# Attention of a hybrid backbone: projections by pairs of heads through DRAM, values two key tiles at a time

## The chip, the cores and the metric

The kernel runs on one core of one Trainium2 chip. The metric is the device time in microseconds (us) of one execution, as the median of several runs. The core has five engines with a queue of instructions each: TensorE (PE, its weight loads PEld), VectorE (DVE), ScalarE (ACT), GpSimd (POOL) and SyncE (SP, which here issues all DMAs). An engine takes its instructions in the order in which the program has them.

## The reference

Two layers run over 1280 tokens (256 of a prompt, 1024 of a sample, which also sees 256 cached keys). Each layer makes one input projection, feeds it to latent attention (8 heads) and to a gated delta rule (GDN, 4 heads, a sequential scan over chunks), gates both, and maps them by one output projection. The change touches the attention:

```
q   = (rmsnorm(q_lat, q_a_norm) @ w_qb).reshape(B, S, H_A, NOPE + ROPE)
q_nope, q_pe = q[..., :NOPE], q[..., NOPE:]            # 64 + 32 per head
ckv = rmsnorm(kv_lat, kv_a_norm)                       # 128 per token, cache appended
kv  = (ckv_all @ w_kvb).reshape(B, -1, H_A, NOPE + V_A)
s = (einsum(q_nope, k_nope) + einsum(q_pe, k_pe)) * scale
o = einsum(softmax(s), v) * silu(g_a)
```

## The kernel before

The program is written as generators ("threads") that record operations. A planner (`Sched`) steps them and decides at build time in which order each engine gets its instructions: it keeps a clock for each engine, takes the thread whose next operation can start first, and breaks ties by the priorities in `PR` (the smaller number goes first). Where the planner's clock has a hole on PE it puts in small filler matmuls (`spare`). The order of the input projection's matrices is the string `ORDER`; of the last `TAIL` matrices token blocks 0 and 1 are done first and block 2 later, so that the buffers of the first blocks come free for the attention.

A layer has three stages. In the first the input projection (`zp`) runs, with the GDN work between. In the second the attention's heads run, with what is left of the GDN scan between. In the third the output projection (`wop`) runs.

For head h, `prep(h)` loads the head's weights (`hw`), multiplies the latent keys and queries (`kp`, `qp`: float32, 64 columns of the array at a time, two blocks side by side), and splits each result into a rounded part hi and a rest lo (ACT and DVE for keys, ACT and POOL for queries). It then finds each query's largest score: 26 matmuls `pm`, each reduced on DVE from PSUM (`at<-pm`), the maxima transposed (`mxt`), scaled on ACT, and sent through DRAM (`mx_d`) into row 96 of the query tile. `main(h)` goes over the key tiles of 128: per tile six `sp` matmuls (hi·hi, hi·lo, lo·hi for two query blocks), an exponential on ACT into `pe`, and, one tile later, the values `po<-pe,vv` (float32, 64 columns, two blocks side by side). POOL and DVE add up the `pe` tiles; at the head's end DVE makes the last addition, and `finish` sums over partitions with two matmuls `pd`, takes the reciprocal, multiplies by the gate on POOL and by `po` on DVE, and writes to DRAM. `prep(h+1)` is paced by flags `m{h}.{tile}` so that its matmuls stand among those of `main(h)`. Key tiles have two slots (`Kt`), and query tiles too (`Q`): head h uses slot h % 2.

Of the kernel before, what the change touches and what calls it, by code (L numbers as in the profile page):

```python
# [16 lines left out]
P = 128  # L17
DM = 1024
# [18 lines left out]
TAIL = 6  # L37
ORDER = 'misc k0 q0 k1 q1 v0 l0 l1 gb0 lk ga0 k2 q2 v1 k3 q3 v2 v3 gb1 gb2 gb3 ga1 ga2 ga3'
PR = dict(ada=2.2, w=2.5, e=2.4, load=2.3, s=1, g=2, p=2.1, kp=2.2, q2=2.2, lat=1, oa=2.45, rope=2.44, prep0=3, prep=3, vv=3, main=4, fin=2, ex=4, red=3, red0=3, prec=5, ldc=4.5, mm=5, fc=1)
VADD = (3, 7, 11)  # L40
# [3 lines left out]
PACE = (0, 0, 0, 1, 2, 3, 4, 4, 5, 6, 7)  # L44
# [12 lines left out]
class Sched:  # L57
# [47 lines left out]
    def run(self):  # L105
        while self.th:
# [115 lines left out]
class Op:  # L222
# [44 lines left out]
    def emit(self):  # L267
        s = self.start()
        if self.eng == "PE":
            n = self.outs[0][0]  # L270
            if (self.half is None) != (Sched.half is None):
                s = max(s, Sched.clk.get("PE", 0.0) + (92 if Sched.half is None else 200))
            if self.half is not None:
                if Sched.half not in (None, (n, self.half)) and Sched.half[0] == n:
                    self.ns = 8
            Sched.half = None if self.half is None else (n, self.half)
# [118 lines left out]
def body(tc, I, O):  # L395
# [74 lines left out]
    qpe_d = dp.tile([2, P, T], F32, name="qpe_d")  # L470
# [88 lines left out]
    def mixer(l, hhl):  # L559
# [315 lines left out]
        def w_thread():  # L875
# [465 lines left out]
        Kt, Q, vvt, at = [], [], {}, {}  # L1341

        def pe_rows(s):
# [3 lines left out]
            ck = bp.tile([P, 2, 32], F32, tag="pe", name="ck", bufs=3) if s else at["ck"]  # L1347
            SY.dma_start(ck, I["cache_kpe"][0, l].rearrange("(c p) f -> p c f", p=P))
# [10 lines left out]
            G.memset(Q[s][1][96:97, :].bitcast(F32), 0.0)  # L1359
            yield 0  # L1360

        def open_attn():
# [5 lines left out]
            o = T + 256  # L1368
            small = t4[:, T:o]
            at.update(ckv=ckv, qn=qn, qr=t4[:, 0:T], hw=[t4[:, o + 192 * i : o + 192 * i + 192].rearrange("p (a b) -> p a b", a=3) for i in range(2)])  # L1370
# [4 lines left out]
            Q.append((t2[:, NK : NK + T], t2[:, NK + T : NK + 2 * T]))  # L1375
            SY.dma_start(ckv[:, 0:T], ckv_d)
            SY.dma_start(qn, qn_d)
            o += 192
            cc = t4[:, o : o + 256].rearrange("p (a b) -> p a b", a=2)
            at["ck"] = t4[:, o + 256 : o + 320].rearrange("p (a b) -> p a b", a=2)  # L1380
            SY.dma_start(cc, I["cache_ckv"][0, l].rearrange("(c p) f -> p c f", p=P))
            sd.add(PR["rope"], rope())
# [6 lines left out]
            yield from pe_rows(0)  # L1389
            sd.add(PR['prep0'], prep(0))  # L1390

        def open_rest():
# [5 lines left out]
            f6 = t6[:, NK:].bitcast(F32)  # L1398
            at["ga"] = [f6[:, 0:640], f6[:, 640:1280]]
            at["ob"] = [bp.tile([P, 512], F32, tag=f"ob{i}", name=f"ob{i}") for i in range(2)]  # L1400
            wv = at["wv"] = bp.tile([P, 512], F32, tag="wv", name="wv")
            SY.dma_start(wv, I["w_v"][l])
            Kt.append((t5[:, 0:NK], t6[:, 0:NK]))
            Q.append((t5[:, NK : NK + T], t5[:, NK + T : NK + 2 * T]))
            for h in range(HA):
                if h:
                    sd.add(PR['prep'], prep(h))
                if h % 2 == 0:
                    sd.add(PR['vv'], vproj(h // 2))
                sd.add(PR['main'], main(h))  # L1410
            sd.add(PR['prec'], pre_c())

        def rope():
# [6 lines left out]
            for g in range(2):  # L1420
# [3 lines left out]
                for b, (c0, n) in enumerate(BLK):  # L1424
# [17 lines left out]
                    SY.dma_start(qpe_d[g, :, c0 : c0 + n], A)  # L1442
# [3 lines left out]
        def vproj(p):  # L1446
            ckv, wv = at["ckv"], at["wv"]
            if p:
                yield f"prep{2*p}"
            vv = vvt[p] = bp.tile([P, NK // P, P], F32, tag="vv", name="vv", bufs=2)  # L1450
            for c0 in (0, 4, 8):
                pt = yield from bank("vp")
                for c in range(4):
                    PE.matmul(pt[:, c * P : (c + 1) * P], ckv[:, (c0 + c) * P : (c0 + c + 1) * P], wv[:, p * P : (p + 1) * P])
# [5 lines left out]

        def prep(h):
            s = h % 2
            ckv, qn = at["ckv"], at["qn"]
            if h:
                yield f"prep{h-1}"
            if h >= 2:
                yield f"main{h-2}"
# [7 lines left out]
            for k0 in (0, 768):
                pt = yield from bank("kp")
                for j in range(2):
                    PE.matmul(pt[64 * j : 64 * j + 64, :384], hw[:, 2, :], ckv[:, k0 + 384 * j : k0 + 384 * j + 384])
                yield 0
                for j in range(2):  # L1480
                    S.copy(kh[0:64, k0 + 384 * j : k0 + 384 * j + 384], pt[64 * j : 64 * j + 64, :384])
                for j in range(2):
                    sl = slice(k0 + 384 * j, k0 + 384 * j + 384)
                    V.tensor_tensor(kl[0:64, sl], pt[64 * j : 64 * j + 64, :384], kh[0:64, sl].bitcast(F32), op=ALU.subtract)
                free(pt)
                yield 0
            hi, lo = Q[s]
            mx, mp = at["mx"][s], at["mp"][s]

            def qproj(bl):  # L1490
                pt = yield from bank("qp")
                for j, b in enumerate(bl):
                    c0, n = BLK[b]
                    for k in range(2):
                        PE.matmul(pt[64 * j : 64 * j + 64, :n], hw[:, k, :], qn[:, k, c0 : c0 + n], start=(k == 0), stop=(k == 1))
                yield 0
                for j, b in enumerate(bl):
                    c0, n = BLK[b]
                    S.copy(at["qr"][0:64, c0 : c0 + n], pt[64 * j : 64 * j + 64, :n])
                free(pt)  # L1500
                for b in bl:
                    c0, n = BLK[b]
                    q = at["qr"][0:96, c0 : c0 + n]
                    S.copy(hi[0:96, c0 : c0 + n], q)
                    G.tensor_tensor(lo[0:96, c0 : c0 + n], q, hi[0:96, c0 : c0 + n].bitcast(F32), op=ALU.subtract)
                yield 0
# [22 lines left out]
            yield from qproj((0,))  # L1529
            yield from mxp(0, 0, 256, mx[:, 0:2], 2)  # L1530
            for b in (1, 2):
                if b == 1:
                    yield from pace(1)
                    yield from qproj((1, 2))
                for t in range(4 * b - 2, 4 * b + 2, 2):
                    for q in (t, t + 1):
                        yield from pace(5 * b - 3 + q - (4 * b - 2))
                        for i, x0 in enumerate((256, 768)):
                            yield from mxp(q, x0, 512, mp[:, q - 2, i : i + 1])
# [370 lines left out]
```

## Time and profile before

| | us |
|---|---|
| median of 3 runs (2219.53 to 2223.38) | 2223.09 |
| profiled execution, its own time | 2217.9 |
| its span, first to last instruction | 2216.1 |
| PE busy | 2097.0 |
| DVE busy | 1442.9 |
| POOL busy | 847.4 |
| ACT busy | 771.0 |

Busy times are unions of instructions of one engine. A matmul's record is longer than the distance to the next matmul, since matmuls are pipelined: what PE needs is read from start to start. A float32 matmul leaves two records. The idle time in brackets stands before an instruction, with the engine or DMA that ended it.

### The profile page before, as it was taken

How to read it: one execution, taken by the hardware profiler on the slowest of the kernel's cores; microseconds unless marked ns; L12 is line 12 of the kernel's file. 1: busy time of each engine (PE TensorE's matmuls, PEld its weight loads, DVE VectorE, ACT ScalarE, POOL GpSimd, SP SyncE). 2: the span in 40 equal slices, each digit the busy share in tenths (PEclk: the TensorE clock that was granted, in tenths of full speed). 3: DMA queues.
4: the chain of work that ended last, by engine and by line, in shares of the span. 5: the costliest groups of instructions: out<-in, count | busy, mean ns of one | idle time of the engine just before them, and what ended most of it. 6: DMA issues, size and time to landing. Idle time of an engine off the chain costs nothing. (4 is left out here: it accounts for less than half of the span.)

```text
span 2216.1 us, 35036 instructions
## 1 busy us (share of the span) xinstructions
PE 2097.0 (95%) x12154; PEld 1519.9 (69%) x12154; DVE 1442.9 (65%) x3085; ACT 771.0 (35%) x2120; POOL 847.4 (38%) x757
## 2 busy tenths in 40 slices
PE   8899999989989998999999999998998999899998
PEld 6676778778666654555777777887876665455576
DVE  4767476686585765564667783887749576665454
ACT  4244224242124344443222441433222434544311
POOL 2343222352415247445331442144341524735521
PEclk9999999989999999999999999999999999999999
DMA  7376776856764322101423654677875441310153
GB/s 276 118 240 196 250 223 194 237 168 209 221 168 150 101 83 71 34 18 50 148 101 95 196 163 151 191 219 216 255 248 158 116 136 53 100 33 19 41 161 110
DMA packets 388481, 327.88 MB, mean 148 GB/s; under 512 B 88736, under 2 KB 326784, under 8 KB 388048
## 3 DMA queue, kind: packets, MB, share of 16 engines
q1 hardware_dynamic: 388304, 325.63, 48.9%
q8 instruction: 97, 1.59, 0.3%
q14 instruction: 80, 0.66, 0.1%
HBM read 220.08 MB, written 105.46 MB: 147 GB/s over the span
## 5 line engine op out<-in xcount | busy, mean ns | idle before, releaser
L312 PE MATMUL zp<-hh,wh 128*128 128x512 f32 (+2 forms) x1128 | 421.5, 374 | 8.4 <-DVE ai L312 6.9
L312 PE MATMUL zp<-hh,wl 128*128 128x512 f32 (+2 forms) x1128 | 421.1, 373 | 4.1 <-POOL wl L312 3.8
L312 PE MATMUL zp<-hl,wh 128*128 128x512 f32 (+2 forms) x1128 | 420.6, 373 | 3.2 <-POOL hl L312 3.1
L312 POOL TENSOR_TENSOR wl<-wr,wh 128x512 fp32r<-128x512 f32 (+1 forms) x114 | 156.2, 1370 | 400.8 <-DVE wh L312 231.5
L312 ACT ACTIVATE pe<-sp 128x512 f32<-128x512 f32 (+1 forms) x352 | 201.6, 578 | 259.0 <-PE sp L312 243.5
L312 DVE TENSOR_REDUCE at<-pm 128x1 f32<-128x512 f32 (+1 forms) x336 | 212.3, 683 | 80.2 <-PE pm L312 79.3
L312 POOL TENSOR_TENSOR pe<-pe,pe 128x1024 f32<-128x1024 f32 x96 | 229.3, 2388 | 80.8 <-DVE pe L312 51.4
L312 PEld LDWEIGHTS zp<-hh,wh 128*128 128x128 f32 (+1 forms) x1128 | 214.1, 190 | 41.9 <-DVE ai L312 7.1
L312 PE MATMUL sp<-at 97*128 97x512 f32 (+1 forms) x704 | 239.9, 408 | 2.6 <-ACT pe L312 1.5
L312 PEld LDWEIGHTS zp<-hh,wl 128*128 128x128 f32 (+1 forms) x1128 | 214.0, 190 | 38.0 <-issue 5.6
L312 PEld LDWEIGHTS zp<-hl,wh 128*128 128x128 f32 (+1 forms) x1128 | 214.2, 190 | 36.3 <-POOL hl L312 4.5
L312 PE MATMUL po<-pe,vv 128*64 128x512 f32 (+1 forms) x768 | 187.1, 563 | 3.4 <-ACT pe L312 2.6
L312 PEld LDWEIGHTS sp<-at 97*128 97x128 f32 x704 | 123.3, 189 | 88.5 <-issue 56.1
L312 POOL TENSOR_SCALAR kpt<-ktok,kdb 128x128 f32<-128x128 f32 x160 | 130.0, 824 | 94.1 <-DMA ai_d<-kpt 84.4
L312 PE MATMUL pm<-at 96*128 96x512 f32 (+1 forms) x416 | 129.2, 385 | 7.9 <-ACT at L312 4.6
L312 PE MATMUL sp<-at,at 97*128 97x512 f32 (+1 forms) x352 | 136.5, 388 | 0.0
L312 DVE TENSOR_TENSOR pe<-pe,pe 128x256 f32<-128x256 f32 (+1 forms) x64 | 79.5, 1244 | 83.9 <-POOL pe L312 43.4
L312 PE MATMUL wop<-woh,ol 128*128 128x512 f32 x288 | 114.4, 397 | 2.2 <-POOL ol L312 2.2
L312 PE MATMUL wop<-woh,oh 128*128 128x512 f32 x288 | 114.5, 398 | 0.0
L312 PE MATMUL wop<-wol,oh 128*128 128x512 f32 x288 | 114.3, 397 | 0.0
L312 PEld LDWEIGHTS pm<-at 96*128 96x128 f32 x416 | 70.9, 191 | 61.5 <-ACT pe L312 21.4
L312 DVE TENSOR_TENSOR wtmp<-blk,W 104x31 f32<-104x31 f32 (+15 forms) x248 | 105.6, 426 | 4.6 <-POOL W L312 0.9
(267 smaller groups left out, 3860.7 us busy)
## 6 DMA issues: line engine op xcount, KB each, us to landing
wr<-in_w_main SPq DMA_DIRECT2D x116, 256.0 KB
ti<-ai_d SPq DMA_DIRECT2D x144, 192.0 KB
ai_d<-ai SPq DMA_DIRECT2D x80, 256.0 KB
kc<-kqv_d SPq DMA_DIRECT2D x160, 128.0 KB
wa<-in_w_ada SPq DMA_DIRECT2D x64, 256.0 KB
kqv_d<-yc SPq DMA_DIRECT2D x48, 256.5 KB
kq<-kqv_d SPq DMA_DIRECT2D x16, 641.0 KB
rb<-grow_d SPq DMA_DIRECT2D x80, 128.0 KB
```

What stands on the lines that cost most here:

```text
L312: op = Op(lambda: f(*a, **k), self.key, self.ns(name, a, k, aps), outs, [x for x in aps if x is not acc])
```

## The change

`proj(p)` now makes keys and queries for a pair of heads at a time, with all 128 columns, splits them in `split` (ACT makes hi; DVE, or POOL where the source isn't PSUM, makes lo) into a staging tile `ev`, and writes both parts to DRAM (`kx_d`, `qx_d`). `loads(h)` reads a head's parts back into its slots. Pair 0 is made with two staging tiles before the heads start, pairs 1 to 3 with one (`at["ev"][:1]`), each from flag `m{2p-2}.5` on. The rotary queries go the same way (`qpe_d` with hi and lo). The hi part of the queries has three slots (`Qh[h % 3]`). `prep(h)` keeps the maxima, now key block by key block. `main` is one thread over all heads; values are multiplied for two key tiles at a time (`PVB`), and a block's `pd` goes with a later group of values than its last one. In `finish` the sums are copied by ACT and the reciprocal is made in pieces of 128. DVE adds one tile (6) and the last of a head, POOL seven. `ORDER` has v0 after lk and ga0 among the tail, and TAIL is 7, so that four more weight tiles are loaded.

```
-TAIL = 6
-ORDER = 'misc k0 q0 k1 q1 v0 l0 l1 gb0 lk ga0 k2 q2 v1 k3 q3 v2 v3 gb1 gb2 gb3 ga1 ga2 ga3'
+TAIL = 7
+ORDER = 'misc k0 q0 k1 q1 l0 l1 gb0 lk v0 k2 q2 v1 k3 q3 v2 v3 gb1 gb2 gb3 ga0 ga1 ga2 ga3'
-VADD = (3, 7, 11)
+VADD = (6,)
+PVB = 2
...
+        def split(x, n):
+            i = at["evn"] = at.get("evn", -1) + 1
+            ev = at["ev"][i % len(at["ev"])]
+            S.copy(ev[:, 0, :n], x)
+            (V if x.space == PSUM else G).tensor_tensor(ev[:, 1, :n], x, ev[:, 0, :n].bitcast(F32), op=ALU.subtract)
+            return ev[:, :, :n].bitcast(F32)
+
+        def proj(p):
+            ckv, qn, hw = at["ckv"], at["qn"], at["hw"]
+            if p:
+                yield "rest"
+                yield f"proj{p-1}"
+                yield f"m{2*p-2}.5"
+            for k0 in range(0, NK, 512):
+                pt = yield from bank("kp")
+                PE.matmul(pt, hw[:, 2, :], ckv[:, k0 : k0 + 512])
+                yield 0
+                SY.dma_start(kx_d[p, :, :, k0 : k0 + 512], split(pt, 512))
+                free(pt)
+            for c0, n in BLK:
...
+                SY.dma_start(qx_d[p, :, :, c0 : c0 + n], split(pt[:, :n], n))
...
+        def loads(h):
+            s, p, g = h % 2, h // 2, h // 4
...
+            if h >= 3:
+                yield f"main{h-3}"
+            yield f"rope{g}"
+            SY.dma_start(qh[64:96].bitcast(F32), qpe_d[g, pe, 0])
+            yield f"proj{p}"
+            SY.dma_start(qh[0:64].bitcast(F32), qx_d[p, rows, 0])
+            for i, (a, b, after) in enumerate(((0, 256, "m{}.0"), (256, 768, "m{}.4"), (768, 1280, "m{}.8"), (1280, NK, "main{}"))):
+                if h >= 2:
+                    yield after.format(h - 2)
+                SY.dma_start(kh[0:64, a:b].bitcast(F32), kx_d[p, rows, 0, a:b])
+                sd.flag(f"kk{h}.{i}")
...
         def prep(h):
-            hw = at["hw"][s]
-            SY.dma_start(hw, I["w_hd"][l, h])
...
             def pace(i):
-                if h:
-                    yield f"m{h-1}.{PACE[i]}"
+                yield f"kk{h}.{i}"
+                if h >= 2:
+                    yield ("m{0}.1", "m{0}.6", "m{1}.0", "m{1}.2")[i].format(h - 2, h - 1)
...
+        def main():
+            todo, done = [], []
+            def pv(n):
+                sums = [b for b in done if b["age"]]
...
+                for x in todo[:n]:
+                    b, kt, m = x["b"], x["kt"], x["b"]["n"]
+                    for y in range(2):
+                        PE.matmul(b["po"][64 * y : 64 * y + 64, :m], vvt[b["h"] // 2][:, kt, b["rows"]], x["pe"][:, y, :m], start=(kt == b["kts"][0]), stop=(kt == b["kts"][-1]))
+                for b in sums:
+                    for y in range(2):
+                        PE.matmul(b["pd"][64 * y : 64 * y + 64, : b["n"]], twos, b["acc"][:, y, :])
...
+                        todo.append(dict(b=blk, kt=kt, pe=pe))
+                        if len(todo) > PVB:
+                            yield from pv(PVB)
```

How PE's order changes is seen first inside a head. Before, in head 5 of the first layer (`at_7079` are its keys and queries, `at_6486` those of head 6, whose maxima `pm` are found meanwhile):

```order
L312 MATMUL sp<-at_7079,at_7080 128x512
L312 MATMUL sp<-at_7079 128x512
L312 MATMUL pm<-at_6486 128x512
L312 MATMUL sp<-at_7079 128x512
L312 MATMUL pm<-at_6486 128x256 x2
L312 MATMUL sp<-at_7079,at_7080 128x512
L312 MATMUL po<-pe,vv 64x512 x2
L312 MATMUL sp<-at_7079 128x512 x2
L312 MATMUL sp<-at_7079,at_7080 128x512
L312 MATMUL sp<-at_7079 128x512 x2
L312 MATMUL sp<-at_7079,at_7080 128x512
L312 MATMUL mxt<-ident,at_6488 10x128
```

A visit to the values (64 columns) came after each key tile, six `sp` apart. Now, in the same head (`at_7352` and `at_7351` are its keys and queries):

```order
L315 MATMUL sp<-at_7351 128x512
L315 MATMUL sp<-at_7352 128x512
L315 MATMUL sp<-at_7352,at_7351 128x512
L315 MATMUL sp<-at_7351 128x512
L315 MATMUL sp<-at_7352 128x512
L315 MATMUL sp<-at_7352,at_7351 128x512
L315 MATMUL sp<-at_7351 128x512
L315 MATMUL sp<-at_7352 128x512
L315 MATMUL sp<-at_7352,at_7351 128x512
L315 MATMUL sp<-at_7351 128x512
L315 MATMUL sp<-at_7352 128x512
L315 MATMUL po<-pe,vv 64x512 x4
```

There are twelve `sp` between visits, each visit has four `po`, and head 6's maxima are no longer among them. In the whole program PE goes into 64-column work and out again 232 times before and 109 times now. The second place is the passage from head 5 to head 6 of the first layer. Before:

```order
L312 MATMUL po<-pe,vv 64x512 x2
L312 MATMUL sp<-at_7079 128x512 x2
L312 MATMUL sp<-at_7079,at_7080 128x512
L312 MATMUL sp<-at_7079 128x512 x2
L312 MATMUL sp<-at_7079,at_7080 128x512
L312 MATMUL po<-pe,vv 64x512 x2
L312 MATMUL vp<-wv,at_6485 128x128 x4
L312 MATMUL po<-pe,vv 64x512 x2
L312 MATMUL pd<-pe_9830,twos 64x512 x2
L312 MATMUL vp<-wv,at_6485 128x128 x8
L312 MATMUL kp<-at_6485,at_6488 64x384 x2
L312 MATMUL sp<-at_6486 128x256 x2
```

Head 6's maxima were complete before head 5's last tile, and its first `sp` follows work that is at hand. Now:

```order
L315 MATMUL sp<-at_7352 128x512
L315 MATMUL po<-pe,vv 64x512 x2
L315 MATMUL pm<-at_6431 128x512 x2
L315 MATMUL po<-pe,vv 64x512 x2
L315 MATMUL pm<-at_6431 128x512 x14
L315 MATMUL pm<-at_6431 128x256 x8
L436 MATMUL spare<-ident 128x128 x30
L315 MATMUL mxt<-ident,at_6433 10x128
L315 MATMUL pm<-at_7351 128x256 x2
L315 MATMUL pm<-at_7351 128x512 x8
L436 MATMUL spare<-ident 128x128 x6
L315 MATMUL sp<-at_6431 128x256 x2
```

All but two of head 6's `pm` now stand behind head 5's last `sp`, then fillers, `mxt`, ten `pm` of head 7, fillers, and head 6's first `sp`. Head 4 has the same form with twelve and six fillers, and the second layer has the same in both places. The third place is SP's queue. Before, at the start of head 5's run:

```order
L312 DMA mx_d0_5_9776<-at4_6488 10x128
L312 DMA at5_7079<-mx_d0_5_9776 1x1280
L312 DMA at4_6488<-in_w_hd 128x192
L312 DMA at4_6488<-qpe_d_101 32x1280
L312 DMA at6_7080<-gates_d_97 64x128
L312 DMA at6_7080<-gates_d_97 64x512
L312 DMA at6_7080<-gates_d_97 64x128
L312 DMA at6_7080<-gates_d_97 64x512
L312 DMA o_d_102<-ob1_7082 64x512 x2
L312 DMA o_d_102<-ob0_7081 64x128 x2
L312 DMA mx_d0_6_10057<-at4_6488 10x128
```

Head 6 needed two loads, weights and rotary queries. Now, in the same stretch (`at2`, `at3` take keys and queries of head 6, `at5`, `at6` of head 7):

```order
L315 DMA at2_6431<-kx_d_102 64x256
L315 DMA at5_7351<-qx_d_103 64x1280
L315 DMA at5_7351<-kx_d_102 64x256
L315 DMA at5_7351<-kx_d_102 64x512 x2
L315 DMA at2_6431<-kx_d_102 64x512 x2
L315 DMA at2_6431<-kx_d_102 64x256
L315 DMA at2_6431<-qpe_d_101 32x1280
L315 DMA at2_6431<-qx_d_103 64x1280
L315 DMA at3_6432<-kx_d_102 64x1536
L315 DMA at5_7351<-kx_d_102 64x256
L315 DMA at5_7351<-qpe_d_101 32x1280
L315 DMA at5_7351<-qx_d_103 64x1280
```

Head 7's keys go into the slot that head 5 is reading, so those loads wait for PE, and the larger part of head 6's keys stands in the queue behind them.

## Rows read from the trace of the kernel before

**Rows 1.** Windows by stage: PE, PEld, DVE, ACT, POOL busy; clock; DMA share.

```profile
624.00:678.00 54.00, 47.16 (x357) 38.33 (x356) 39.02 (x102) 18.13 (x52) 5.30 (x8) 0.97 0.65 177
678.00:1035.00 357.00, 346.22 (x1705) 196.85 (x1703) 213.51 (x341) 164.71 (x350) 185.13 (x110) 0.99 0.24 70
1730.00:2093.00 363.00, 350.10 (x1724) 198.85 (x1724) 215.63 (x342) 165.85 (x356) 185.14 (x112) 0.99 0.25 72
```

**Rows 2.** Timeline of PE in head 5 and 6: start, length, what.

```profile
961.30 1.08 PE L312 MATMUL po<-pe,vv 128*64 128x512 f32 x4
962.30 0.73 PE L312 MATMUL sp<-at 97*128 97x512 f32 x2
962.88 0.40 PE L312 MATMUL sp<-at,at 97*128 97x512 f32 x1
963.11 0.62 PE L312 MATMUL sp<-at 97*128 97x512 f32 x2
963.57 0.40 PE L312 MATMUL sp<-at,at 97*128 97x512 f32 x1
963.89 1.08 PE L312 MATMUL po<-pe,vv 128*64 128x512 f32 x4
964.90 1.16 PE L312 MATMUL vp<-wv,at 128*128 128x128 f32 x8
...
969.84 0.87 PE L312 MATMUL kp<-at,at 128*64 128x384 f32 x4
970.64 0.50 PE L312 MATMUL sp<-at 97*128 97x256 f32 x2
...
974.68 1.03 PE L312 MATMUL qp<-at,at 128*64 128x256 f32 x4
975.63 0.73 PE L312 MATMUL sp<-at 97*128 97x512 f32 x2
...
979.37 1.94 PE L312 MATMUL qp<-at,at 128*64 128x512 f32 x8
981.24 0.72 PE L312 MATMUL sp<-at 97*128 97x512 f32 x2
```

**Rows 3.** Timeline of PE, a float32 product with all 128 columns.

```profile
577.69 1.13 PE L312 MATMUL rp<-at,wpe 128*128 128x256 f32 x4
578.47 0.58 PE L312 MATMUL zp<-hh,wh 128*128 128x512 f32 x1
```

**Rows 4.** Timeline, end of head 2 in the first layer.

```profile
836.90 4.96 POOL L312 TENSOR_TENSOR wol<-wor,woh 128x512 fp32r<-128x512 f32 x4
836.98 7.62 DVE L312 TENSOR_TENSOR pe<-pe,pe 128x1024 f32<-128x1024 f32 x3 [6.92 <-POOL pe L312]
844.32 1.98 PE L312 MATMUL pd<-pe,twos 128*64 128x512 f32 x4 [5.47 <-DVE pe L312]
```

**Rows 5.** Timeline, end of a head in the second layer.

```profile
1897.97 1.97 PE L312 MATMUL pd<-pe,twos 128*64 128x512 f32 x4 [5.26 <-DVE pe L312]
```

**Rows 6.** Instructions by tile: count, duration ns min/median/max, first and last start.

```profile
L312 DVE TENSOR_REDUCE at<-pm x336: 675/681/694, 633.2 to 2056.7; 128x1 f32<-128x512 f32 x128, 128x2 f32<-128x512 f32 x40
L312 DVE TENSOR_TENSOR pe<-pe,pe x64: 361/1224/5956, 685.5 to 2095.9; 128x1024 f32<-128x1024 f32 x48, 128x256 f32<-128x256 f32 x16
L312 POOL TENSOR_TENSOR pe<-pe,pe x96: 2355/2378/2849, 694.9 to 2092.1; 128x1024 f32<-128x1024 f32 x96
L312 ACT COPY vv<-vp x24: 566/585/603, 638.7 to 2025.0; 128x512 f32<-128x512 f32 x24
L312 DVE TENSOR_TENSOR ra<-rp,rt x8: 671/683/693, 582.3 to 1672.3; 128x512 f32<-128x512 f32 x8
```

**Rows 7.** Timeline of the maxima's way into the query tile, head 4, first layer.

```profile
884.05 0.28 PE L312 MATMUL mxt<-ident,at 128*10 128x128 f32 x1
...
884.66 0.30 SPq L312 DMA_DIRECT2D mx_d<-at  x1
...
885.96 0.23 SPq L312 DMA_DIRECT2D at<-mx_d  x1
...
888.33 0.48 PE L312 MATMUL sp<-at 97*128 97x256 f32 x2
```

**Rows 8.** Waits of SP's queue for landings: us in total, times, longest.

```profile
SPq L312 <- DMA mx_d<-at: 16.8, 15, 2.9
SPq L312 <- DMA ai_d<-ai: 8.4, 8, 3.1
SPq L312 <- DMA xs<-x: 6.0, 1, 6.0
```

More of the change, by code (lines that the diff above doesn't have):

```diff
@@ L272, in emit @@
                 s = max(s, Sched.clk.get("PE", 0.0) + (92 if Sched.half is None else 200))
[L273 to L276, printed above, removed]
+            if self.half is None:
+                Sched.half = None
+            elif Sched.half and Sched.half[0] == n and self.half not in Sched.half[1]:
+                self.ns = 8
+                Sched.half[1].add(self.half)
+            else:
+                Sched.half = (n, {self.half})
         e = s + self.ns
@@ L1358, in pe_rows @@
             G.memset(lo[96:97, :].bitcast(F32), 0.0)
-            G.memset(Q[s][1][96:97, :].bitcast(F32), 0.0)
+            G.memset(Ql[s][96:97, :].bitcast(F32), 0.0)
             yield 0
+        def split(x, n):
[17 more added lines that the diff above has]
+            for c0, n in BLK:
+                pt = yield from bank("qp")
+                for k in range(2):
+                    PE.matmul(pt[:, :n], hw[:, k, :], qn[:, k, c0 : c0 + n], start=(k == 0), stop=(k == 1))
+                yield 0
+                SY.dma_start(qx_d[p, :, :, c0 : c0 + n], split(pt[:, :n], n))
+                free(pt)
+            if p + 1 < HA // 2:
+                SY.dma_start(hw, I["w_hd"][l, p + 1])
+            yield 0
+            sd.flag(f"proj{p}")
         def open_attn():
@@ L1389, in open_attn @@
             yield from pe_rows(0)
+            sd.add(PR["rope"], rope())
+            for p in range(HA // 2):
+                sd.add(PR['projs' if p else 'proj'], proj(p))
+            sd.add(PR['prep0'], loads(0))
             sd.add(PR['prep0'], prep(0))
@@ L1475, in prep @@
[L1475 to L1486, printed above, removed]
@@ L1487, in prep @@
-            hi, lo = Q[s]
-            mx, mp = at["mx"][s], at["mp"][s]
[L1490 to L1506, printed above, removed]
+            kh, hi = Kt[s][0], Qh[h % 3]
@@ L1612, in main, with finish @@
                 yield 0
-            sd.flag(f"main{h}")
-        def finish(h, po, acc, m, c0, n, ga):
+        def finish(b):
+            h, c0, n, ga, po, pd = (b[q] for q in ("h", "c0", "n", "ga", "po", "pd"))
             p, e = h // 2, h % 2
             i = at["n"] = at.get("n", -1) + 1
-            if i >= 2:
-                yield f"ob{i-2}"
-            pd = yield from bank("pd")
-            for x in range(2):
-                PE.matmul(pd[64 * x : 64 * x + 64, :n], twos, acc[:, x, :n])
-            yield 0
-            ob = at["ob"][i % 2]
-            V.reciprocal(ob[:, :n], pd[:, :n])
+            j = i % len(at["ob"])
+            ob, rc, user = at["ob"][j], at["rc"][j], at.get(("user", j))
+            at["user", j] = f"ob{i}"
+            if user:
+                yield user
+            V.tensor_tensor(ob[:, :n], po[:, :n], ga, op=ALU.mult)
+            free(po)
+            S.copy(rc[:, :n], pd[:, :n])
@@ L1626, in finish @@
             free(pd)
             yield 0
-            G.tensor_tensor(ob[:, :n], ga, ob[:, :n], op=ALU.mult)
+            for x in range(0, n, P):
+                V.reciprocal(rc[:, x : x + P], rc[:, x : x + P])
+                yield 0
+            G.tensor_tensor(ob[:, :n], ob[:, :n], rc[:, :n], op=ALU.mult)
             yield 0
-            V.tensor_tensor(ob[:, :n], po[:, :n], ob[:, :n], op=ALU.mult)
-            free(po)
             for x in range(2):
@@ L1641, in pre_c @@
             yield f"done{HB-1}"
+            yield "rest"
             gs.close()
+            b2 = open_pool(bs, f"b2{l}", bufs=1, side="right")
+            for t in ("ob", "rc"):
+                at[t].append(b2.tile([P, 512], F32, tag=t, name=t))
             cw = open_pool(cs, f"cw{l}", bufs=1)
```

228 lines of the change are left out of this document (122 added, 106 removed).

## The prediction

> **What bounds the kernel now.** I read the windows by stage first. In both attention stages PE is busy in 97% and 96% of the stretch (346.22 of 357.00, 350.10 of 363.00), and DVE, POOL and ACT in 46% to 60% [rows 1]. So the attention is bound by PE, and the change is worth what it takes off PE's path, less the waits that it puts there. The 54 us in front of the first attention stage have 7 us without PE [rows 1].
>
> Then I read PE's own order from start to start. Two `sp` stand 0.46 us apart from the next two (963.11 to 963.57), 0.23 each. From one visit to the values to the next, with six `sp` between, it is 2.59 us (961.30 to 963.89) [rows 2]. Six times 0.23 is 1.38, so the visit costs 1.21. Its arithmetic is 0.86: eight `qp` records take 1.87 (979.37 to 981.24), four `po` records 1.01 (963.89 to 964.90), and the second four add the difference [rows 2]. Hence 0.35 us of each visit is passage: 0.09 on the way in (0.32 from the last `sp` to `po` instead of 0.23), 0.15 on the way out (1.01 instead of 0.86), and 0.12 at the first two `sp` (0.58 instead of 0.46) [rows 2].
>
> Last I looked for PE's long holes in the attention. The two longest are `pd` waiting for DVE's last addition of a head, 5.47 and 5.26 us [rows 4, 5].
>
> **The change part by part.** The sum is made against the profiled execution, 2217.9 us (span 2216.1).
>
> Visits. PE goes into 64-column work 232 times before and 109 times now, 123 fewer. At 0.34 (0.35 is from 512-column visits, some are shorter) that is 41.8 us less, nearly all in the two stages where PE is the bound. Bounds: only the way out, 0.15, saves 18; all of 0.36 (0.09 + 0.15 + 0.12) saves 44.
>
> Projections. Keys cost the same: before, two visits a head of 0.80 less the way out, 0.65 each, so 1.30 [rows 2]; now three products of 512 with all columns, 0.86 each, serve two heads, 1.29 a head. Queries cost 0.95 - 0.15 = 0.80 plus 1.87 - 0.15 = 1.72, together 2.52 a head [rows 2]; now one product of 256 (two halves, 0.78 [rows 3]) and four of 512 at 0.86, 4.22 a pair, 2.11 a head. Sixteen heads save 6.6 us. The way into and out of full-width float32 seems free: 0.78 holds both [rows 3]. Bounds 0 and 6.6.
>
> The sums `pd`. They now go with a later group of values, some ten `sp` on, about 2.3 us at the least and in most heads longer, and behind them stands work of the next head. The holes of 5.47 and 5.26 go, 10.7 us; what is late next is `finish`, which has a whole head for it. In rows: DVE's addition starts at 836.98 beside four POOL instructions from 836.90 on [rows 4] and takes up to 5956 ns instead of 1224 [rows 6]. The Trainium skill, "SBUF — State Buffer", section "SBUF: two separate sides", calls the port pair of VectorE and GpSimd an exclusive lock: who starts first holds it for the instruction and the other blocks. The rows agree: DVE finished only behind POOL's run. By that rule DVE's delay stays, since `wol` and seven additions a head are POOL's, and if the maxima's reduces behind it held PE as long, this term would be 0; by the rows PE waited for `pd` alone, so I keep 10.7 and 0 as the other bound.
>
> Loads and staging. This is what is added. From the middle of head 2p-2, six blocks go through one staging tile: ACT 0.59, DVE 0.68 [rows 6], a write to DRAM, and only then the next block's ACT copy. No row has a write of 512 KB with its landing alone. The nearest waits are 2.9 us at the longest for a small write, 3.1 for one of 256 KB and 6.0 for one of 512 KB [rows 8]; I take 3.1, and with 0.5 for the passes between engines a block takes 4.9 us and a pair 29. From head 4's first `sp` to head 6's it is 82.3 us (888.33 to 970.64 [rows 2, 7]), 41 a head, now some 38; so with 19 us of head 2p-2 left, pair p is ready about 10 us into head 2p-1.
>
> Idle at head 6. In SP's queue the larger part of head 6's keys stands behind loads into head 5's slot, which wait until PE has read head 5's tile 9. From there: SP issues and a landing, 3.4 us (2.4 is the longest that a small read can have taken, 885.96 to 888.33 [rows 7], and 1.0 for issues); twenty reduces of 0.68, 13.6 [rows 6], with 3 us of DVE's other work between; `mxt` to the first `sp`, 4.3 (884.05 to 888.33 [rows 7]). That is 24.3 us. PE has in it two key tiles (12 `sp`, 2.8), two visits with four `po` (4.1), 26 `pm` (16 at 0.23 and ten half as long, 4.9) and ten `pm` of head 7 (2.1): 13.9. So about 10 us are idle. Before, all of this lay beside head 5's matmuls.
>
> Idle at head 4. Its key loads come a step earlier, so only four reduces and the way of the maxima stand open: 2.7 + 0.2 + 4.3, less 3.1 of `pm`, is 4.1; ahead of it two more sets of fillers among head 4's first `pm` mark a hole behind the projection, for which I take another 4. Head 2 has GDN work to fill. So 18 us a layer, 36 in all. Bounds: 9 (in both places only the way of the maxima, 4.3 less 2.1 of `pm`) and 60 (10 at each of heads 2, 4 and 6).
>
> Costs at nothing. DVE makes one pe addition of 1.22 fewer a head, the reciprocals and splits come to about the same; POOL's one more of 2.38 [rows 6] takes the place of the three query splits that it loses; ACT does less: all stay near 60% of a shorter stage. SP gets 178 more DMAs in the whole run, at some 0.3 us of issue (0.30, 0.23 [rows 7]), nearly all in stages whose DMA engines are 24% busy [rows 1]; what that costs is the order, counted above. Four more weight tiles and v0 four matrices later lie beside `zp`, which fills PE. Pair 0's products replace head 0's; I take 0 for the passage, with 7 either way, the idle time there.
>
> Sum: 2217.9 - 41.8 - 6.6 - 10.7 + 36 = 2194.8. The median of the runs shown, 2223.09, is 5.2 above the profiled execution; on that footing the forecast is 2200.
>
> **The rivals.**
> First, the new idle time is small: DVE and SP run ahead of the planner's clock, and only 9 us stay. 2200 - 27 = 2173. For it: DVE has 40% free. Against: the queue's order is fixed, and the reduces' 13.6 us cannot start sooner.
>
> Second, the passage is cheaper and DVE stays locked: visits save 25 (0.20 each, between 0.15 and 0.34), `pd` nothing. 2223.1 - 25 - 6.6 + 36 = 2227, about no change. For it: the period also holds reduces' and exponentials' waits. Against: the same 0.32 and 1.01 stand at both visits shown [rows 2].
>
> Third, slower: the staging tile. If a write takes the 6.0 us of [rows 8], a block takes 7.8 and a pair 47, 18 us later. Each of the two exposed heads a layer starts that much later, four times 18 = 72: 2272. It decides from 23 / 4, some 6 us a pair or 1 us a block, on. For it: ACT and DVE take the block's copies in order among exponentials and reduces, and I gave that 0.5. Against: the 6.0 is a single wait [rows 8]; here the DMA engines are at 24% [rows 1].
>
> That the visits don't become fewer is no rival: PE's order shows it.
>
> **How the numbers follow.** The forecast, 2200 (2183 to 2216), gets 0.48; the first rival, below 2183, 0.19; the second, 2216 to 2234, 0.16; the third, above, 0.17. This measurement tells 0.2% from no change, 4.4 us. Faster than 2218.6: 0.48 + 0.19 + 0.05 of the second = 0.72. Within: 0.09. Slower than 2227.5: 0.19. The range for 8 in 10 goes from 2168, a little under the first rival, to 2242, part of the third's way.
>
> **What would show it.** Right: some 345 us instead of 357 from the first `sp` to the first `wop` of a layer, and 350 instead of 363 in the second; visits of eight `po` records in about 2.1 us; no `pd` with more than 1 us idle before it; idle of 4 and 10 us before `mxt` and the first `sp` of heads 4 and 6, with DVE in reduces without a break, and SP waiting for PE. Wrong: `po` visits of over 2.4 us; ACT held at the staging tile for more than 5 us a block; idle time also at heads 2, 3, 5 or 7; or a first attention stage that starts much later than at 678.

## The result, and the profile after

The changed kernel takes 2248.6 us (median of 4 runs, 2245.3 to 2254.1), before 2222.5 in the same series: ratio 1.0127, 95% interval 1.0103 to 1.0151. It is slower by some 26 us; 2200 (2168 to 2242) was forecast. The profiled execution spans 2244.3 us, 28.2 more than before.

I cut both spans at the start of the last `zp`, the first `sp` and the first `wop` of the first layer, and at the start of the first and last `zp`, the first `sp` and the first `wop` of the second; the pieces of a row add up to the span. What stands ahead of the first `zp` counts to the first stage.

| kernel | first `zp` stage | passages, last `zp` to first `sp` | `zp`, second layer | attention, both | output, both | span |
|---|---|---|---|---|---|---|
| before | 623.7 | 54.4 + 54.1 | 511.0 | 720.0 | 252.8 | 2216.1 |
| after | 616.1 | 74.4 + 61.8 | 523.2 | 708.8 | 260.0 | 2244.3 |

The attention stages got 11 us shorter, and 39 are lost outside them: 28 in the passages, 12 in the second `zp`, 7 in the output projections, less 8 in the first `zp`. Some 10 of the 28 are waiting: in the passages PE idles 16.8 us instead of 12.5 and runs fillers for 11.3 instead of 5.8. The rest is work that moved. All rotary products `rp` stood beside `zp` before; now half of them, 19 us of PE, stand behind the last `zp`. The 12.4 us of keys and queries that stood there before went ahead of it, and some GDN products came over from the attention. The line of `rp` in before, then its windows in the two passages of after:

```profile
L312 PE MATMUL rp<-at,wpe x80: 377/592/697, 577.7 to 1671.3; 128*128 128x512 f32 x64, 128*128 128x256 f32 x16
```
```profile
616.00:690.50 74.50, 10.65 (x20) 4.52 (x20) 2.75 (x4) 0.37 (x1) 0.93 0.87 243
1702.00:1763.80 61.80, 8.33 (x20) 3.56 (x20) 2.76 (x4) 0.37 (x1) 0.96 0.90 241
```

The windows of the two attention stages, to be laid beside [rows 1], and behind them the fillers alone (the line of `spare`: length, PE and PEld busy, clock, DMA share, GB/s):

```profile
690.00:1045.00 355.00, 339.31 (x1670) 216.16 (x1671) 196.96 (x332) 145.45 (x311) 178.53 (x93) 0.98 0.41 118
1763.00:2117.00 354.00, 339.14 (x1713) 216.26 (x1713) 197.98 (x340) 144.55 (x307) 179.01 (x96) 0.98 0.43 121
```
```profile
690.00:1045.00 355.00, 23.20 (x160) 22.78 (x160) 0.98 0.41 118
1763.00:2117.00 354.00, 17.14 (x122) 16.92 (x122) 0.98 0.43 121
```

PE's busy share hides the loss, since fillers count as busy and a low clock makes work look longer. So I split a stage into idle time (length less busy), fillers, time lost to the clock ((1 - granted clock) times length), and the rest, PE's own work. The clock column has two digits, so each clock term is good to about 2 us. Of before, the fillers of the two stages are 6.75 and 4.66.

| attention, both layers | length | idle | fillers | clock | lost in all | PE's own work |
|---|---|---|---|---|---|---|
| before | 720.0 | 23.7 | 11.4 | 7.2 | 42.3 | 677.7 |
| after | 709.0 | 30.6 | 40.3 | 14.2 | 85.1 | 623.9 |

The work fell by 54, and 43 came back as lost time. The visits look as forecast: PE's timeline in head 5 (as [rows 2]) has eight `po` records in 1.87 us, 0.32 from the last `sp` to `po`, and 0.34 from the first `sp` behind them to the next:

```profile
957.33 0.61 PE L315 MATMUL sp<-at 97*128 97x512 f32 x2
957.88 1.94 PE L315 MATMUL po<-pe,vv 128*64 128x512 f32 x8
959.75 0.50 PE L315 MATMUL sp<-at,at 97*128 97x512 f32 x1
960.09 0.64 PE L315 MATMUL sp<-at 97*128 97x512 f32 x2
```

The lost time stands where the next pair begins. PE's timeline from the end of head 5 to head 6's first `sp`, with DVE's maxima beside it:

```profile
969.09 8.77 PE L315 MATMUL pm<-at 96*128 96x512 f32 x22
977.66 7.82 PE L436 MATMUL spare<-ident 128*128 128x128 f32 x60
985.32 0.27 PE L315 MATMUL mxt<-ident,at 128*10 128x128 f32 x1
985.34 2.95 PE L315 MATMUL pm<-at 96*128 96x256 f32 x10
988.13 1.50 PE L436 MATMUL spare<-ident 128*128 128x128 f32 x12
989.39 0.49 PE L315 MATMUL sp<-at 97*128 97x256 f32 x2
```
```profile
968.56 12.04 DVE L315 TENSOR_REDUCE at<-pm 128x1 f32<-128x512 f32 x20
980.64 0.18 DVE L315 TENSOR_REDUCE at<-at 128x8 f32<-128x24 f32 x1
```

A line of a timeline can merge two sizes: the 22 `pm` are 14 of 512 columns and eight of 256, the next ten are two of 256 and eight of 512. The 22 take 8.6 us at DVE's pace (12.04 / 20 = 0.60 us a reduce) instead of 4.2 at 0.23 and half of it, the fillers 7.7 and 1.3, the ten 2.8 instead of 2.1: some 14 us without use. For 4.5 of them the fillers hold PE beyond their cause: the maxima were done at 980.82, and `mxt` stands behind the fillers until 985.32.

Why so late? PE's first `sp` of head 4 and first product of pair 3, ACT's first pass of each block of the pair through the one staging tile, and SP's loads behind the last block:

```profile
902.28 0.35 PE L315 MATMUL sp<-at,at 97*128 97x256 f32 x1 [0.25 <-DVE at L315]
...
918.68 1.12 PE L315 MATMUL kp<-at,at 128*128 128x512 f32 x2
```
```profile
919.85 0.59 ACT L315 CAST at<-kp 128x512 fp32r<-128x512 f32 x1 [0.78 <-PE kp L315]
926.75 0.58 ACT L315 CAST at<-kp 128x512 fp32r<-128x512 f32 x1
932.43 0.58 ACT L315 CAST at<-kp 128x512 fp32r<-128x512 f32 x1
938.08 0.37 ACT L315 CAST at<-qp 128x256 fp32r<-128x256 f32 x1
943.72 0.59 ACT L315 CAST at<-qp 128x512 fp32r<-128x512 f32 x1 [0.28 <-PE qp L315]
950.20 0.59 ACT L315 CAST at<-qp 128x512 fp32r<-128x512 f32 x1 [1.32 <-PE qp L315]
```
```profile
955.91 0.49 SPq L315 DMA_DIRECT2D at<-qx_d  x1
956.50 2.47 SPq L315 DMA_DIRECT2D o_d<-ob  x4
959.01 0.60 SPq L315 DMA_DIRECT2D at<-kx_d  x1
959.65 0.60 SPq L315 DMA_DIRECT2D at<-qx_d  x1
960.60 3.65 SPq L315 DMA_DIRECT2D at<-kx_d  x6
```

A block takes 6.1 us ((950.20 - 919.85) / 5). The pair starts 16 us into head 4, which now lasts only 30 us, and its last block has landed when SP reads it back at 955.91, some 23 us into head 5 (first `sp` at 932.35). From there SP issues the loads of heads 6 and 7 one behind the other, with no pause of more than 0.4 us: none of them waits for PE.

Head 4 is no better. There the first hole is a wait for the keys' landing, with a low clock behind it (0.62 granted from 870 to 875); 24 and 12 more filler records follow:

```profile
867.24 0.77 PE L315 MATMUL pm<-at,at 96*128 96x256 f32 x2 [3.33 <-DMA at<-kx_d]
...
870.01 4.22 PE L436 MATMUL spare<-ident 128*128 128x128 f32 x20
...
896.75 0.28 PE L315 MATMUL mxt<-ident,at 128*10 128x128 f32 x1 [2.73 <-DVE at L315]
```

The `pd` holes of [rows 4, 5] are gone from the heads. One of more than 1 us is left, where a head's last sum stands among the output projection of the second layer:

```profile
2125.10 1.08 PE L315 MATMUL pd<-pe,twos 128*64 128x512 f32 x4 [2.91 <-DVE pe L315]
```

### The profile page after: what moved, and what is told of

Same layout as the page of the kernel before. It is cut to its first block, busy times and chain, and to the rows that moved or that the text cites. A ratio compares the mean times of both kernels' runs of the same rounds, so it can differ in the third digit from the quotient of the medians.

```text
span 2244.3 us, 35296 instructions
## 1 busy us (share of the span) xinstructions
PE 2101.7 (94%) x12158; PEld 1570.2 (70%) x12158; DVE 1438.6 (64%) x3105; ACT 739.7 (33%) x2052; POOL 858.1 (38%) x741
## 4 chain that ended last, share of the span: by engine, by line
PE 41%; DVE 15%; DMA 12%; issue 3%; POOL 3%; SPq 3%; ACT 2%; DVEq 0%; POOLq 0%; ACTq 0%
PE wop L315 9%; PE sp L315 7%; PE po L315 6%; PE zp L315 6%; DVE at L315 3%; SPq L315 3%; PE pm L315 2%; DVE wtmp L315 2%; DVE W L315 2%; POOL pe L315 2%; DVE yc L315 2%; DMA at<-kx_d 1%; PE px L315 1%; DMA wr<-in_w_main 1%; DMA qx_d<-at 1%
## 5 line engine op out<-in xcount | busy, mean ns | idle before, releaser
L315 POOL TENSOR_TENSOR pe<-pe,pe 128x1024 f32<-128x1024 f32 x112 | 267.5, 2388 | 283.3 <-PE po L315 213.4
L315 PE MATMUL sp<-at 97*128 97x512 f32 (+1 forms) x572 | 196.3, 400 | 1.2 <-DVE ob L315 0.9
L315 PE MATMUL sp<-at,at 97*128 97x512 f32 (+1 forms) x484 | 186.9, 410 | 1.3 <-ACT vv L315 0.9
L315 PE MATMUL po<-pe,vv 128*64 128x512 f32 (+1 forms) x704 | 163.0, 578 | 0.3 <-ACT pe L315 0.2
L315 PEld LDWEIGHTS sp<-at 97*128 97x128 f32 x572 | 103.8, 190 | 35.6 <-issue 16.6
L315 PEld LDWEIGHTS sp<-at,at 97*128 97x128 f32 x484 | 91.5, 190 | 34.7 <-issue 11.3
L315 DVE SCALAR_TENSOR_TENSOR yc<-zp_sb,cwh,yc 128x256 f32<-128x256 f32 (+1 forms) x144 | 103.6, 719 | 4.1
L315 PE MATMUL wop<-woh,ol 128*128 128x512 f32 x256 | 101.9, 398 | 1.6 <-POOL ol L315 1.6
L315 PE MATMUL wop<-woh,oh 128*128 128x512 f32 x256 | 102.0, 398 | 0.0
L315 DVE RECIPROCAL rc<-rc 128x128 f32<-128x128 f32 x80 | 70.0, 920 | 47.7 <-ACT rc L315 47.6
```

Of the source, the lines that this page charges most:

```text
L315: op = Op(lambda: f(*a, **k), self.key, self.ns(name, a, k, aps), outs, [x for x in aps if x is not acc])
```

## The experiments

In the names, `a_` is the kernel after with one edit or several, `b_` the kernel before with one; `a_pE` has the projections earlier. The medians are of 4 to 10 runs, and the ratio is to before in the same series.

| kernel | median us | ratio to before, 95% interval | passages | `zp`, layer 2 | attention |
|---|---|---|---|---|---|
| a_oldorder | 2262.8 | 1.0195 (1.0155 to 1.0234) | 81.2 + 77.4 | 516.6 | 709.7 |
| b_neworder | 2256.0 | 1.0147 (1.0118 to 1.0176) | 43.1 + 52.4 | 524.1 | 763.0 |
| a_rope | 2255.0 | 1.0143 (1.0112 to 1.0173) | 68.5 + 58.2 | 535.7 | 697.7 |
| a_pvb1 | 2247.6 | 1.0112 (1.0074 to 1.0149) | 73.9 + 60.2 | 527.8 | 710.8 |
| a_pE | 2217.6 | 0.9975 (0.9958 to 0.9991) | 74.3 + 62.5 | 523.7 | 671.5 |
| a_pE_pvb1 | 2236.1 | 1.0060 (1.0038 to 1.0081) | 74.8 + 59.9 | 524.0 | 697.0 |
| a_pE_tail6 | 2197.3 | 0.9884 (0.9861 to 0.9907) | 62.8 + 61.0 | 526.2 | 658.0 |
| a_ev2x | 2240.6 | 1.0078 (1.0051 to 1.0104) | 74.4 + 62.5 | 534.7 | 704.1 |
| a_tail6 | 2252.8 | 1.0145 (1.0110 to 1.0180) | 64.2 + 58.9 | 525.8 | 710.6 |
| a_mxq | 2255.2 | 1.0156 (1.0124 to 1.0187) | 73.9 + 65.3 | 520.5 | 715.5 |
| a_pE_t6_ld1 | 2203.4 | 0.9920 (0.9892 to 0.9948) | 58.9 + 55.4 | 525.2 | 670.4 |
| a_nofill | 2254.3 | 1.0154 (1.0125 to 1.0184) | 73.0 + 62.6 | 530.2 | 705.4 |
| a_ev1 | 2295.1 | 1.0321 (1.0279 to 1.0362) | 94.8 + 104.9 | 516.9 | 709.0 |
| a_pE_t6_proj | 2186.5 | 0.9823 (0.9791 to 0.9856) | 59.5 + 67.1 | 525.2 | 643.2 |

**The order, in both kernels.** `ORDER` and `TAIL` exchanged between the two kernels.

> The kernel after with ORDER and TAIL of the kernel before (v0 and ga0 early, tail of 6), all else as changed. Theory A (the order is what the start of the attention lost): the first sp comes back from 690.5 and 1763.8 us to about 680 and 1732, and the time falls from 2248.6 to some 2220 to 2225. Theory B (the way of pair 0 and of the rotary queries through DRAM is what it lost): the order is worth nothing, the first sp stays within 5 us of 690 and 1764, and the time stays at 2243 to 2254. Theory C (the heads themselves lost it): as B, no change ahead of the first sp.

> The kernel before with ORDER and TAIL of the kernel after, nothing else. Theory A: the time rises from 2222.5 to some 2240 to 2250, with the first sp 12 us later in layer 0 and 30 us later in layer 1, and the stages between the first sp and the first wop unchanged. Theory B and C: 2218 to 2228.

No theory came out. The kernel before gets some 32 us slower with the new order, more than theory A's price and not in its way: the first `sp` of layer 0 comes 19 us earlier, not later, the passages get 13 shorter, and the attention, which was to stay, 43 longer. The kernel after gets 14 slower with the old order, where theory A had it faster and the others the same. The two don't add: the order is worth a loss of some 32 in one program and a gain of 14 in the other. The second `zp` goes the same way both times: 511.0 becomes 524.1, and 523.2 becomes 516.6. So much of its 12 us goes with the order; but with one and the same order the other edits put it anywhere from 516.9 to 535.7, so the order isn't all of it. The passages follow the rest of the change: 108.5 and 95.5 with the old way of pair 0, 158.6 and 136.2 with the new.

**The rotary queries first.** `sd.add(PR["rope"], rope())` moved back to where the kernel before has it.

> The kernel after with the thread of the rotary queries added where the kernel before adds it (ahead of the key rows and of pair 0's projections). Theory B: the 52 fillers and the 3.3 us wait for wpe at 616 to 626 us go, as does part of the same wait in layer 1, and the time falls by 9 to 20 us, to 2229 to 2240. Theory A: the rotary products only change places with other work, 2243 to 2254. Theory C: as A.

Theory B's price is refuted. What it names is real, as PE's timeline of after shows behind the last `zp`:

```profile
616.32 5.97 PE L436 MATMUL spare<-ident 128*128 128x128 f32 x52
625.60 2.05 PE L315 MATMUL rp<-at,wpe 128*128 128x256 f32 x4 [3.32 <-DMA wpe<-in_w_qpe]
```

The passages get 9.5 shorter, but the first `zp` ends 10 later and the second takes 12 more: of the 40 rotary records in the passages 8 are left, and the work stands beside `zp` again. With them gone the passages are still 18 us longer than before the change.

**The price of a visit.**

```
-PVB = 2
+PVB = 1
```

> The kernel after with PVB = 1: values for one key tile at a time again, some 230 visits to 64-column work instead of 109, and fewer fillers at heads 4 and 6 (216 in all instead of 271). With 0.34 us a visit, as the prediction had it, the attention stages get some 42 us longer, less some 16 us of idle time that goes at heads 4 and 6: 2274. With 0.20 us a visit (what the stage of after suggests: 24 us fewer in po for 120 visits fewer): 25 less 16, 2257. If the idle time at heads 4 and 6 is what eats the gain altogether, 2248 or below.

The third case: 92 visits more (201 instead of 109) cost nothing. Its windows of the attention, and the fillers:

```profile
688.00:1038.00 350.00, 339.52 (x1612) 199.56 (x1611) 191.07 (x333) 146.21 (x311) 178.16 (x93) 0.99 0.42 119
1758.00:2119.00 361.00, 346.28 (x1658) 202.02 (x1656) 192.80 (x341) 144.57 (x303) 175.85 (x96) 0.98 0.42 119
```
```profile
688.00:1038.00 350.00, 12.56 (x100) 12.04 (x100) 0.99 0.42 119
1758.00:2119.00 361.00, 9.48 (x72) 8.82 (x72) 0.98 0.42 119
```

Idle 25.2, fillers 22.0, clock 10.7: 57.9 lost instead of 85.1, and 653.1 of work instead of 623.9. So a visit costs 29.2 / 92 = 0.32 us of PE's work, and the holes had hidden all of it.

**The projections earlier.**

```
-                yield f"m{2*p-2}.5"
+                yield f"m{max(2*p-3,0)}.{0 if p==1 else 4}"
```

> The kernel after with the projections of pairs 1 to 3 set free earlier: flag m0.0 for pair 1 and m{2p-3}.4 (the head before, tile 6) for pairs 2 and 3, instead of m{2p-2}.5. Theory D (the holes ahead of heads 4 and 6 are the end of the pair's chain projection, DRAM, maxima, which starts too late): idle time, fillers and low clock of the two attention stages fall from 85 us to some 45, heads 3 and 5 take about 48 and 43 us instead of 63 and 57, and the time falls by 35 to 50 us, to 2200 to 2213. Theory E (the holes come from head 6's key loads behind head 7's in SP's queue, and from the reduces on DVE, whenever the pair is ready): at most 10 us, 2238 to 2250.

Theory D, with 31 us in place of 35 to 50. The windows and fillers:

```profile
693.00:1021.00 328.00, 315.67 (x1523) 194.43 (x1519) 200.35 (x331) 143.96 (x311) 176.67 (x93) 0.99 0.46 127
1741.00:2084.00 343.00, 323.91 (x1590) 198.82 (x1589) 202.53 (x341) 145.69 (x312) 177.57 (x97) 0.98 0.44 125
```
```profile
693.00:1021.00 328.00, 2.21 (x16) 2.01 (x16) 0.99 0.46 127
1741.00:2084.00 343.00, 0.39 (x2) 0.30 (x2) 0.98 0.44 125
```

Idle 31.4, fillers 2.6, clock 10.1: 44.1 lost instead of 85.1, nearly as little as before the change, with the same work (626.9). Heads 3 and 5 of layer 0 take 44.6 and 33.5 us instead of 63.0 and 57.0. Theory E's price is refuted. The planner makes the order of every queue anew, SP's too, so this run alone doesn't part the earlier start from the new order; that no load of SP waits for PE in the lines of after above speaks against SP's queue as well.

> The kernel a_pE with PVB = 1, values for one key tile at a time. If the visits cost what PE's own times say once no hole hides them (some 29 us of work between the two kernels with and without, 0.24 us a visit), it is 25 to 33 us above a_pE. By the prediction's 0.34 it would be 42 above. If another chain than PE's bounds the heads (as with the late projections, where PVB = 1 cost nothing), it is within 8 us of a_pE.

18.5 above a_pE: less than either price, but far from free. With 97 more visits (207 instead of 110) the attention is 25.5 longer, 0.26 us a visit; the other stages give some of it back. Once the chain is early, PE bounds the heads again and the visits pay.

**The staging tile.** Pairs 2 and 3 get a second tile in the place of the second `ob` and `rc`:

```
-            for t in ("ob", "rc"):
-                at[t].append(b2.tile([P, 512], F32, tag=t, name=t))
+            at["ev"].append(b2.tile([P, 2, 512], F32R, tag="ev2", name="ev2"))
```

> The kernel after with a second staging tile for pairs 2 and 3 from the end of the GDN work on, in the place of the second pair of tiles ob and rc. Theory D': it is the one staging tile that makes the chain late (a block every 6 us): pair 3 takes some 18 us instead of 34, the hole ahead of head 6 goes, that ahead of head 4 stays, and the time falls by 10 to 20 us, to 2228 to 2238. Theory E: within 5 us of after.

Head 5 falls from 57.0 and 57.4 to 45.8 in both layers, as theory D' says, and head 3 stays at 63.5 and 59.8. Of these 23 us 8 are left, under the 10 to 20 expected: the last heads, which lost a tile, take 31.9 instead of 27.9, the second `zp` is 11 longer, the output projections, without the last head's `po` and `pd`, 11 shorter.

**The tail.** `TAIL = 6`, first with the early projections (a_pE_tail6), then alone (a_tail6):

> The kernel a_pE with TAIL = 6 (four weight tiles fewer are loaded and split, block 2 of ga0's neighbour done early), order of matrices as changed. If the longer tail is what made the input projection of the second layer 12 us longer, 8 to 15 us below a_pE, with zp of layer 1 at some 512 us; if it is not, within 5 us of a_pE.

> The kernel after with TAIL = 6 alone. Theory F (the tail of 7 is a loss by itself, whatever the heads do, as a_pE_tail6 against a_pE suggests with its 20 us): 15 to 25 us below after, 2224 to 2234, with the first sp of layer 0 near 684. Theory G (the 20 us came from how the shorter tail meets the early projections): within 8 us of after, 2240 to 2257.

With them it gives 20 us, and not in the second `zp` (526.2), so that reason is refuted; alone it gives nothing (theory G). The gain over a_pE is in the first passage (11.5) and in the attention (13.5).

**SP's queue.** In after, head 0's maxima are scaled at 673.3 and their write is issued at 681.5, behind 11 other DMAs. In a_mxq ACT issues it:

```
+            Q = AD if h < 2 else SY
+            Q.dma_start(md.rearrange("o (t f) -> (o t) f", f=P), mt)
+            Q.dma_start(hi[96:97, :].bitcast(F32), md)
```

> The kernel after with the way of the maxima through DRAM (mx_d, its write and its read) issued by ACT instead of SP for heads 0 and 1; the order of every other instruction stays. Theory H (the start of the attention is late because head 0's maxima stand behind 11 other DMAs in SP's queue, 8.2 us in layer 0 and 3.1 us in layer 1): the first sp comes some 8 us and 3 us earlier and the time falls by 8 to 14 us. Theory I (PE reaches the first sp only after the GDN products that stand ahead of it, and these wait for their own loads): first sp within 3 us of 690 and 1764, the time within 5 us of after.

The timeline of a_mxq:

```profile
671.68 0.56 ACTq L315 DMA_DIRECT2D mx_d<-at  x1
673.01 0.23 ACTq L315 DMA_DIRECT2D at<-mx_d  x1
...
687.53 0.50 PE L315 MATMUL sp<-at 97*128 97x256 f32 x2
```

The maxima's read is issued 11 us earlier than in after (684.23), and the first `sp` comes 3.0 and 1.5 earlier, since GDN products stand ahead of it on PE until 687.5: theory I for the first `sp`. So in after head 0's maxima hold up the first `sp` by 3 us at most. The time is 6.6 up, outside its 5; the second attention stage got 9 longer, and I can't say why.

On a_pE_tail6, head 1's loads were then held back (`yield "m0.0"` in `loads(1)`; a_pE_t6_ld1):

> The kernel a_pE_tail6 with head 1's loads held back to head 0's first tile (flag m0.0), so that SP issues some nine DMAs fewer ahead of the first sp, where it issues 67 to 72 per cent of the time in after. If SP's queue is what holds up the GDN loads there (theory J): the first sp 3 to 6 us earlier in each layer, and the time 4 to 12 us below a_pE_tail6. Otherwise within 5 us of it.

The passages are 9.5 shorter, the attention is 12 longer, the whole 6 slower. Theory J is refuted in its total.

**The fillers.** Left out between the start and the end of the heads (`Sched.spin` does nothing there):

> The kernel after without the filler matmuls from the start of the heads to their end (120 instead of 271 in all; every other instruction keeps its order). Theory K (at head 6 the 30 fillers hold PE 4.5 us beyond the last maximum in each layer, and 6 more stand ahead of its first sp): 9 to 13 us below after, 2235 to 2240. Theory L (without them the granted clock falls in the holes, and what follows runs at the low level): the holes get shorter by as much, but the clock's loss in the attention stages rises from 16 us to 25 or more, and the time stays at 2244 to 2258.

Theory L, by its time and by the clock: without fillers the clock falls. The same ten microseconds at head 6, first of after, then of this kernel:

```profile
980.00:990.00 10.00, 9.90 (x78) 8.92 (x77) 4.92 (x10) 0.27 (x1) 0.00 (x0) 1.00 0.06 18
```
```profile
980.00:990.00 10.00, 6.95 (x24) 5.34 (x22) 9.00 (x16) 1.04 (x3) 0.00 (x0) 0.56 0.12 34
```

Head 5 gets 4.4 and 4.9 shorter, while the stages' clock is 0.94 and 0.96 (35 us lost, 21 more than in after). So the fillers held PE, and leaving them out gained nothing.

**The start of the attention.** One staging tile from the start on (`at["ev"]` without its second tile), and the order of its two users turned round (`proj=2.0` instead of 2.445, on a_pE_tail6; a_pE_t6_proj):

> The kernel after with one staging tile instead of two ahead of the heads too (rotary queries and pair 0 share it); what follows has one tile already. Theory M (the way of pair 0 and of the rotary queries through the staging tiles sets the passage from the input projection into the heads): some 18 blocks wait for one tile, 2 to 3 us more each: both passages get 15 to 40 us longer (from 74 and 62 us), and the time rises by 30 to 70 us, to 2280 to 2320. Theory I (GDN products and their loads set the passage): within 10 us of after.

> The kernel a_pE_tail6 with pair 0's projection ahead of the rotary queries in the planner's priorities (2.0 instead of 2.445). If pair 0's blocks waiting behind the rotary ones for the two staging tiles are what makes the passages long (theory M): 5 to 15 us below a_pE_tail6, both passages shorter by 3 to 8 us. If all blocks of both are needed in any order: within 6 us of a_pE_tail6.

One tile makes the passages 20 and 43 us longer, the first `zp` 12 and the second 6 shorter, and the time 46 longer: theory M's price, the 43 a little above it. With one tile the staging carries the passage; that it does with two isn't shown by this. The second is the fastest of all, 10.8 under a_pE_tail6, but not for theory M's reason: the passages are 3 longer, and the attention is 15 shorter.

```profile
688.00:1010.00 322.00, 312.63 (x1503) 194.42 (x1501) 191.30 (x325) 141.73 (x295) 173.94 (x92) 0.98 0.47 130
1735.00:2057.00 322.00, 315.44 (x1564) 193.93 (x1561) 197.69 (x336) 142.50 (x296) 175.13 (x94) 0.99 0.48 133
```

Idle 15.9, clock 9.7, almost no fillers: 26 lost. PE's own work, 618, is nearly that of after; what went is the lost time. The attention is 77 us shorter than in before, and the kernel is faster than both: 2186.5, with before at 2223.0 in the same series.

## Why the prediction was wrong

**Visits and projections: right.** 41.8 and 6.6, 48.4 together, were forecast; the attention's own work fell by 53.8 (head 1's products, now made with pair 0 ahead of the heads, and some GDN products, now in the passages, are a part). a_pvb1 gives 0.32 us of PE's work a visit where the rows gave 0.34. Once PE bounds the heads, a_pE_pvb1 against a_pE gives 0.26 in the attention and some 0.2 in the whole time. So the price of PE's work was right; the second rival's 0.20 is too low for it, but near what the whole time paid.

**The sums `pd`: nearly right.** 10.7 forecast; the holes are gone from the heads, 2.9 and 0.7 came back at the output projections. The case by the Trainium skill's rule of the lock ("SBUF — State Buffer", section "SBUF: two separate sides"), 0, didn't come. The trace agrees with the rule itself: DVE's additions, which answer to the second line of [rows 6], still stretch beside POOL's work, up to 3357 ns instead of 5956, but no sum in the heads waits for one; the longest is the one behind the 2.9 us:

```profile
L315 DVE TENSOR_TENSOR pe<-pe,pe x32: 1161/1224/3357, 716.0 to 2121.7; 128x1024 f32<-128x1024 f32 x32
```

**Idle time at heads 4 and 6: mis-sized, the first step that failed.** Forecast were 36 more, or 25 with the `pd` holes that go; measured are 43 more lost. The failing step is "pair p is ready about 10 us into head 2p-1": it is 23. A block takes 6.1 us, not 4.9, which is 8 us a pair, and head 2p-2 lasts 30 us, not 38, which leaves 14 us of it instead of 19, since the maxima that had stood in it now stand behind head 2p-1. Around the holes themselves stand two costs that had no term, fillers that hold PE beyond the last maximum (4.5 us at head 6, though a_nofill, without them, was no faster) and the lower clock (7 us more). a_pE shows the cause: only the flag that starts the pairs is moved, and 41 of the 43 are gone; a_ev2x, where a second tile has pair 3's last block read back at 944.45, 9 us into head 5, takes 11 us off head 5 in both layers. Not SP's queue behind head 5's slot, as I had put it, but the pair's late end decided: no load of heads 6 and 7 waited for PE there. That the planner's new order around the earlier flag has no part in the 41 isn't shown.

**The third rival** named this chain. By its own arithmetic 1.2 us a block is 7 a pair and 28 in four places, 2228; the staging was given too little weight, though not as the whole of the loss.

**"Costs at nothing": the second step that failed, and the larger one.** The passage stood at 0, 7 either way, and four weight tiles and v0 at 0. Measured are 39 us outside the attention: 28 in the passages, 12 in the second `zp`, 7 at the output, 8 gained in the first `zp`. The prediction's own sign of error, a first stage much later than at 678, came: 690.5. The step took pair 0's products to replace head 0's in the passage. They don't: they went ahead of the last `zp`, and in their place came half of the rotary products, which the sum nowhere had; a_rope shows the exchange from the other side. Why so many rotary products come behind the last `zp` is shown in part: with one staging tile instead of two, which they share with pair 0, it is 28 records a passage instead of 20, and the passages are 20 and 43 longer (a_ev1). Whether a third tile would bring the 28 us back wasn't tried, and which of the rotary queries, the GDN products and head 0's loads has which part of the rest stays open. Of the 12 in the second `zp` a large part goes with the order of the matrices, 13 and 7 in the two kernels.

The sum: 5 better in the work, 18 worse in the holes, 39 unseen: some 52, the distance from 2194.8 to 2246.5, the profiled execution's own time.

## What to carry to other kernels

Where a change takes work off a bound engine, ask which chain becomes the bound next, and give that chain its start before looking at the gain: here 29 us of PE's work paid nothing until one flag was moved. Count fillers and the clock's loss as lost time, since both hide in a busy share of 96%. A detour through DRAM has a period for each buffer (6 us a block here): with one buffer less, two stage starts took 20 and 43 us more. And before a term is put at nothing, ask of every product that the change reroutes where it will stand: half of the rotary products left their place beside `zp` without being counted.

## What the runs showed of the hardware

A hole can cost the clock behind it too. In the first output projection of after PE is idle for 2.46 us from 1079.8 on, and then runs at the lower level, 1.2 of 2.4 GHz, for a while:

```profile
1082.29 1.11 PE L315 MATMUL htp<-ident,xn 128*128 128x128 f32 x4 [2.46 <-DVE xn L315]
```
```profile
1080.00:1082.00 2.00, 0.00 (x0) 0.00 (x0) 0.83 (x3) 0.43 (x2) 0.56 (x1) 1.00 0.88 262
1082.00:1084.00 2.00, 1.71 (x6) 1.58 (x7) 1.53 (x3) 0.56 (x2) 0.00 (x0) 0.51 0.91 335
1084.00:1086.00 2.00, 2.00 (x7) 1.56 (x6) 0.98 (x2) 1.56 (x5) 0.00 (x0) 0.63 0.65 194
```

The two later stretches lose 1.7 us ((0.49 + 0.37) x 2). By the mean granted clock of the spans, 0.986 and 0.980, the clock lost 31 us before and 45 after, 14 more. This is an upper bound on its part of the 28 us, since a part falls on time in which PE had nothing to do.
